# Low parts of more weight slabs made in the first feed-forward stage and kept in DRAM

## Chip, core and metric

The kernel runs on one core of a Trainium2 chip. The metric is the device time of one execution in microseconds; the median of the runs counts. A profile of one execution comes from the hardware profiler. Its engines are called by two names here: PE is TensorE (matmuls), PEld its weight loads, DVE is VectorE, ACT is ScalarE, POOL is GpSimd, and SP is SyncE, whose queue issues all the DMAs (SPq).

## What is computed

Two blocks of two layers each, on 512 tokens of width 1024, all in fp32. A layer of the first block, cut to what matters here:

```python
h = x @ w_in[i]                       # queries, keys, values of three attentions, an index, and gates g
o_fox, o_sb, o_dsa = ...              # forgetting, stick-breaking and top-k attention
gates = sigmoid(g.reshape(b, s, 3, 1024))
merged = gates[:, :, 0] * (o_fox @ w_up_fox[i]) + gates[:, :, 1] * (o_sb @ w_up_sb[i]) + gates[:, :, 2] * (o_dsa @ w_up_dsa[i])
x = layer_norm(ALPHA * x + merged @ w_out[i])
ffn = square(relu(x @ w_ff_in[i])) @ w_ff_out[i]        # 1024 -> 4096 -> 1024
ple = sigmoid(x @ w_ple_gate[i]) * (p[i] @ w_ple[i])
x = layer_norm(ALPHA * x + ffn + ple)
```

The second block (`block2`) has its own `w_in_2` and other mixers. It matters here because part of its weights is prepared during the first block.

## The kernel before, in words

**Three matmuls for one.** Each fp32 operand is split into a high part (the value rounded to the fp32r format that TensorE reads) and a low part (the rest). `mm3` (lines 213 to 215) multiplies high by high, high by low and low by high. A weight slab is 128 partitions x 1024 words, that is four row blocks of 128 by 256 columns, 512 KB. `slab` (line 224) loads it into the tile `raw` on SyncE's queue. `wsplit` (lines 237 and 238) makes the tiles `wh` on ScalarE (a copy that rounds) and `wl` on VectorE (raw less high), or on GpSimd where `lo_on_pool` is set. `raw`, `wh` and `wl` have four buffers each.

**Projections.** `w_tiles` takes output tiles of 128 columns in pairs: two slabs for a pair (the upper and the lower half of the 1024 rows), 24 matmuls of 512 tokens for a tile, and then `emit` does the tile's follow-up work. `wide` does the other kind of product, with four blocks of tokens held in PSUM.

**The order of a layer** (`block1`): `mix1`, `out1`, `ffn`. In `mix1` the string ORDER, 'ISFDftdxBbzy', gives the traced order: index projection (I), scores of the selection (S), projections of the forgetting (F) and of the top-k attention (D), the attentions (f, d, b), the top-k search on VectorE (t), the stick-breaking projection (B), and the three gate branches (x, z, y). The stages I (its second group), D and F have their low parts on GpSimd, by LOP = "iDF". The queries and keys of F and B come through `head_pairs`, the gates through `branch`, both by `w_tiles`. On each engine the framework's scheduler orders the instructions ahead of the run, by traced order and readiness under its own cost estimates; in the run each engine takes its list in that order.

**Low parts in advance.** The feed-forward stage `ffn` runs in four chunks: eight output tiles by `w_tiles` (relu and square, `emit_h`), then the two halves of the second product by `wide`. After each output tile it runs one step of the list `ahead`. A step (`lows2`, lines 256 to 263) loads a slab of the second block's `w_in_2` into `lraw`, copies it to `llo` on ScalarE (line 259), subtracts on GpSimd (line 260) and stores the low part in DRAM (line 263), into a tile of its own. `lraw` and `llo` have two buffers each. `issue_after` puts a step's load behind the latest slab's load in SyncE's queue. There are 24 steps in each of the first block's two layers (one for each layer of the second block), so three of the four chunks carry eight steps and the last none. In the second block `stored` loads the low part from DRAM into `wl` (line 272) where a tile's columns are in the list, and only the high part is computed (line 273).

Of the kernel before, what the change touches and what calls it, by code (L numbers as in the profile page):

```python
# [19 lines left out]
P = 128  # L20
# [3 lines left out]
KD = D // P  # L24
# [45 lines left out]
class Net:  # L70
# [171 lines left out]
        pairs = [[(3352 + j * P, P), (2840 + j * P, P)] for j in range(4)] + [[(1816 + j * 256, 256)] for j in range(2)]  # L242
        return pairs + [[(1304 + j * P, P), (1304 + (j + 2) * P, P)] for j in range(2)] + [[(c + j * 256, 256)] for c in (2328, 3864) for j in range(2)]

    def lows2(self, l):

        nc, w = self.nc, self.a["w_in_2"][l]
        kept = self.lows[l] = {}

        def step(cols, k0):  # L250
            c = sum(n for _, n in cols)
            raw, lo = self.t("lraw", [P, 4, c]), self.t("llo", [P, 4, c], F32R)
            o = 0
            with self.tc.issue_after(self.last_load.ins):
                for c0, n in cols:
                    nc.sync.dma_start(raw[:, :, o:o + n],
                                      w[k0 * P:(k0 + 4) * P, c0:c0 + n].rearrange("(k p) c -> p k c", p=P))
                    o += n
            nc.scalar.activation(lo, raw, AF.Copy)  # L259
            nc.gpsimd.tensor_sub(lo, raw, lo.bitcast(F32))  # L260
            n = self.name("low")
            kept[tuple(cols), k0] = self.dp.tile([P, 4, c], F32, tag=n, name=n)
            nc.sync.dma_start(kept[tuple(cols), k0], lo.bitcast(F32))

        return [lambda cols=cols, k0=k0: step(cols, k0) for cols in self.gates2(l) for k0 in (0, 4)]

    def stored(self, w, cols, k0, nk, lows):

        raw = self.slab(w, cols, k0, nk)
        hi, lo = self.t("wh", raw.shape, F32R), self.t("wl", raw.shape, F32R)  # L270
        with self.tc.issue_after(self.hold):
            self.nc.sync.dma_start(lo.bitcast(F32), lows[tuple(cols), k0])
        self.nc.scalar.activation(hi, raw, AF.Copy)
        return hi, lo

    def w_tiles(self, w, tiles, x, emit, K=KD, lows=None):

        for j0 in range(0, len(tiles), 2):
            pair = tiles[j0:j0 + 2]
            cols = _merge([p for t in pair for p in t])  # L280
            ks = self.KS[self.block]
            if ks == 8:
                raw = self.slab(w, cols, 0, K)
                parts = [[self.wpair(raw[:, :, j * P:(j + 1) * P])] for j in range(len(pair))]
            else:
                slabs = [self.stored(w, cols, k0, ks, lows) if lows else self.wpair(self.slab(w, cols, k0, ks))
                         for k0 in range(0, K, ks)]
                parts = [[(h[:, :, j * P:(j + 1) * P], l[:, :, j * P:(j + 1) * P]) for h, l in slabs] for j in range(len(pair))]
            for j in range(len(pair)):
                ps = self.ps("mm")  # L290
                for k in range(K):
                    h, l = parts[j][k // ks]
                    self.mm3(ps, (h[:, k % ks], l[:, k % ks]), (x[0][:, k], x[1][:, k]), k == 0, k == K - 1)
                emit(j0 + j, ps)
# [305 lines left out]
    def head_pairs(self, w, tiles, x):  # L600


        q, k = {}, {}

        def pair():
            t = self.t("qk", [P, 2, T], F32R)
            return t[:, 0], t[:, 1]

        def emit(i, ps):
            j = i // 2  # L610
            ps = self.staged(ps)
            if i % 2:
                for r in range(2):
                    k[2 * j + r] = pair()
                    self.key_stack(ps, *k[2 * j + r], 64 * r)
                return
            z = pair()
            last = i == len(tiles) - 1
            for r in range(1 if last else 2):
                self.query_stack(ps, z[r], 64 * r, 64 * r)  # L620
                q[2 * j + r] = z[r], z[r]
            if last:
                k[2 * j] = pair()
                self.key_stack(ps, *k[2 * j], 64)

        self.w_tiles(w, tiles, x, emit)
        return q, k

    def forget(self, ffl, b_forget):
# [100 lines left out]
    def branch(self, w, g0, wup, pairs, rows, x, emit):  # L730

        nc = self.nc
        nk = len(pairs)
        full = rows // P
        ups = {}

        def gate(f, ps):
            if f % 2 == 0:
                raw = self.t("raw", [P, nk, 256])
                c = slice(f * P, f * P + 256)  # L740
                nc.sync.dma_start(raw[:, :full], wup[:full * P, c].rearrange("(k p) c -> p k c", p=P))
                h, l = self.t("wh", raw.shape, F32R), self.t("wl", raw.shape, F32R)
                if full < nk:
                    nc.sync.dma_start(raw[:64, full], wup[full * P:, c])
                    self.split(raw[:64, full], h[:64, full], h[64:, full])
                self.wsplit(raw[:, :full], h[:, :full], l[:, :full])
                ups[0] = h, l
            h, l = ups[0]
            s = self.t("sig", [P, T])
            nc.scalar.activation(s, ps, AF.Tanh, scale=0.5)  # L750
            u = self.ps("mm")
            c = slice(f % 2 * P, f % 2 * P + P)
            if full < nk:
                nc.tensor.matmul(u, h[:, full, c], pairs[full][:, 0], start=True, stop=False)
                nc.tensor.matmul(u, h[:, full, c], pairs[full][:, 1], start=False, stop=False)
            for k in range(full):
                self.mm3(u, (h[:, k, c], l[:, k, c]), (pairs[k][:, 0], pairs[k][:, 1]),
                         k == 0 and full == nk, k == full - 1)
            emit(f, s, u)

        self.w_tiles(w, [[(g0 + f * P, P)] for f in range(KD)], x, gate)

    def mix1(self, i, x, then=None):

# [165 lines left out]
    def ffn(self, i, x, y, pt, post=None):  # L930
        nc = self.nc
        a = self.a
        ple = {}
        for j in range(2):
            def emit(b, ps):
                if b == 0:
                    ple[j] = self.wpair(self.slab(a["w_ple"][i], [(j * T, T)], 0, 2))
                wh, wl = ple[j]
                s = self.t("sig", [P, T])
                nc.scalar.activation(s, ps, AF.Tanh, scale=0.5)  # L940
                u = self.ps("mm")
                tok = slice(b * P, (b + 1) * P)
                for k in range(2):
                    self.mm3(u, (pt[0][:, k, tok], pt[1][:, k, tok]), (wh[:, k], wl[:, k]), k == 0, k == 1)
                nc.vector.scalar_tensor_tensor(s, s, 1.0, u, op0=OP.add, op1=OP.mult)
                v = y[b][j]
                nc.vector.scalar_tensor_tensor(v, v, ALPHA, s, op0=OP.mult, op1=OP.add)

            self.wide(a["w_ple_gate"][i], j * T, x, emit, stay=1)
        xo = self.xpair()  # L950
        xn = self.dram([T, D])
        nch = 4
        ahead = self.lows2(i)
        for ch in range(nch):
            hid = []

            def emit_h(f, ps):
                r = self.t("sig", [P, T])
                nc.scalar.activation(r, ps, AF.Relu)
                nc.vector.tensor_mul(r, r, ps)  # L960
                t = self.t("qk", [P, 2, T], F32R)
                self.split(r, t[:, 0], t[:, 1])
                hid.append(t)
                self.run(ahead, 1)

            self.w_tiles(a["w_ff_in"][i], [[(ch * D + f * P, P)] for f in range(KD)], x, emit_h)
            m = _Stack(hid, 0), _Stack(hid, 1)
            last = ch == nch - 1
            if last:
                g, bb = self.bcast(a["ln2_g"][i], D), self.bcast(a["ln2_b"][i], D)  # L970

                st = self.stats()

            def add(j):
                def emit(b, ps):
                    v = y[b][j]
                    nc.vector.tensor_add(v, v, ps)
                    if last:
                        nc.vector.bn_stats(st[b][:, j], v)
                    if last and j == 1:  # L980
                        self.norm_out(y[b], b, st[b], g, bb, 1e-5, xo, xn, post)
                return emit

            self.out_halves(a["w_ff_out"][i][ch * D:(ch + 1) * D], m, add)
        return xo, xn
# [21 lines left out]
    def block1(self, layers=DEPTH, post=None):  # L1007
        self.phase(1, self.FIRST)
        xd = self.a["x"]
        x, rest = self.load_x()  # L1010
        for i in range(layers):
            merged = self.mix1(i, x, None if i else rest)
            if i == 0:
                self.tables = self.rope_tables()
            pt = self.ple_input(i)
            x, y = self.out1(i, merged, xd)
# [672 lines left out]
```

## Time and profile before

| | us |
|---|---|
| median of 3 runs | 2550.74 |
| lowest and highest run | 2550.54, 2554.34 |
| the profiled execution's own time | 2551.98 |
| its span, first to last instruction | 2550.2 |
| TensorE busy in the span | 2472.7 |
| VectorE, ScalarE, GpSimd busy | 1630.3, 1231.7, 729.7 |

The profiled execution is 1.2 us above the median, and its time is 1.8 us longer than its span. All times in the rows below count from the span's start. The stages in that time: the first layer's feed-forward stage proper lies at 486 to 862 us (its first steps are issued at 488.5), the second layer's mixing block at 870 to 1270, its feed-forward stage from about 1372 on, and the second block begins near 1738. TensorE's busy time is modelled from pipelined matmuls, so idle time in it is real, but a busy TensorE isn't always at its peak.

### The profile page before, as it was taken

To read this page: it belongs to the slowest core of one execution; us is meant where nothing else is said; L and a number is where in the kernel's file an instruction comes from. 1 tells how busy PE (TensorE), PEld (TensorE's weight loads), DVE (VectorE), ACT (ScalarE), POOL (GpSimd) and SP (SyncE) were. 2 spreads that over 40 slices of the span, in tenths; PEclk is the share of its full clock that TensorE was granted. 3 is DMA by queue.
4 is the path that set the end of the run, shared out by engine and by line. 5 is a ranking of instruction groups with operands and counts; after the bars stand their busy time and mean duration, and the time that the engine had idled before them with its cause. 6 is when DMAs were issued, how large, how long until landed. Compare 5 with 4: busy or idle time off the path is not lost.

```text
span 2550.2 us, 35074 instructions
## 1 busy us (share of the span) xinstructions
PE 2472.7 (97%) x12660; PEld 2097.7 (82%) x12660; DVE 1630.3 (64%) x3126; ACT 1231.7 (48%) x2271; POOL 729.7 (29%) x845
## 2 busy tenths in 40 slices
PE   8989999999999998999999999998999899999998
PEld 8878888888888887888888888887988688988777
DVE  4985865654344669659465544346699755589874
ACT  5665643344333255665323343233575742576760
POOL 5621560122110264206002122004353312353320
PEclk9999999999999999999999999999999999999999
DMA  5203225366543332132435656334444143554151
GB/s 167 83 16 85 74 83 187 123 197 224 170 161 94 96 85 66 46 86 82 133 119 169 203 190 222 93 97 121 140 143 130 43 150 114 149 153 127 51 178 40
DMA packets 276654, 312.00 MB, mean 122 GB/s; under 512 B 25792, under 2 KB 221696, under 8 KB 276480
## 3 DMA queue, kind: packets, MB, share of 16 engines
q1 hardware_dynamic: 276480, 309.76, 39.4%
q8 instruction: 100, 1.64, 0.3%
q14 instruction: 74, 0.61, 0.1%
HBM read 274.84 MB, written 34.87 MB: 121 GB/s over the span
## 4 chain that ended last, share of the span: by engine, by line
PE 82%; DVE 9%; ACT 3%; DMA 2%; issue 2%; POOL 1%; SPq 0%; DVEq 0%; ACTq 0%; POOLq 0%
PE mm L214 19%; PE mm L215 18%; PE mm L213 18%; PE ss L382 3%; PE av L432 3%; PE ss L214 3%; PE ss L215 3%; PE ss L213 3%; PE tr L417 2%; PE av L215 1%; PE av L214 1%; PE av L213 1%; PE tr L215 1%; PE tr L214 1%; PE tr L213 1%
## 5 line engine op out<-in xcount | busy, mean ns | idle before, releaser
L238 DVE TENSOR_TENSOR wl<-raw,wh 128x1024 fp32r<-128x1024 f32 (+3 forms) x308 | 392.8, 1279 | 326.9 <-ACT wh L237 317.9
L237 ACT ACTIVATE wh<-raw 128x1024 fp32r<-128x1024 f32 (+6 forms) x358 | 361.3, 1013 | 448.8 <-PE tr L215 176.9
L213 PE MATMUL mm<-xt,wh 128*128 128x512 f32 x1456 | 574.4, 394 | 2.1 <-DVE sig L1376 2.1
L215 PE MATMUL mm<-xt,wl 128*128 128x512 f32 x1456 | 572.2, 393 | 2.8 <-DVE wl L238 2.8
L214 PE MATMUL mm<-xt,wh 128*128 128x512 f32 x1456 | 573.8, 394 | 0.0
L215 PEld LDWEIGHTS mm<-xt,wl 128*128 128x128 f32 x1456 | 275.0, 189 | 59.0 <-DVE wl L238 4.4
L213 PEld LDWEIGHTS mm<-xt,wh 128*128 128x128 f32 x1456 | 275.1, 189 | 57.3 <-DVE sig L1376 2.5
L214 PEld LDWEIGHTS mm<-xt,wh 128*128 128x128 f32 x1456 | 274.9, 189 | 54.5 <-issue 0.5
L260 POOL TENSOR_TENSOR llo<-lraw,llo 128x1024 fp32r<-128x1024 f32 x48 | 116.3, 2435 | 378.3 <-ACT llo L259 363.4
L213 PE MATMUL mm<-wh,xt 128*128 128x256 f32 (+6 forms) x624 | 190.4, 311 | 10.1 <-ACT wh L237 8.8
L215 PE MATMUL mm<-wh,xt 128*128 128x256 f32 (+6 forms) x624 | 191.9, 310 | 5.8 <-DVE xt L206 5.7
L214 PE MATMUL mm<-wl,xt 128*128 128x256 f32 (+6 forms) x624 | 192.6, 311 | 2.4 <-DVE wl L238 1.6
L364 POOL TENSOR_SCALAR tiny<-tiny 128x1 f32<-128x1 f32 x24 | 11.9, 495 | 516.7 <-DVE tiny L863 477.7
L391 ACT ACTIVATE s<-s,tm 128x128 f32<-128x128 f32 (+1 forms) x216 | 120.5, 558 | 64.4 <-DVE tm L389 57.2
L214 PE MATMUL mm<-wl,qk 128*128 128x512 f32 x352 | 136.2, 390 | 0.0
L215 PE MATMUL mm<-wh,qk 128*128 128x512 f32 x352 | 136.0, 389 | 0.0
L213 PE MATMUL mm<-wh,qk 128*128 128x512 f32 x352 | 134.7, 389 | 0.0
L394 POOL TENSOR_SCALAR s<-s,tm,kept 128x128 f32<-128x128 f32 (+3 forms) x128 | 78.4, 612 | 195.0 <-DVE tm L393 174.0
L213 PEld LDWEIGHTS mm<-wh,xt 128*128 128x128 f32 x624 | 119.6, 194 | 12.8 <-ACT wh L237 9.2
L215 PEld LDWEIGHTS mm<-wh,xt 128*128 128x128 f32 x624 | 120.4, 193 | 8.3 <-DVE xt L206 7.2
L214 PEld LDWEIGHTS mm<-wl,xt 128*128 128x128 f32 x624 | 120.7, 194 | 5.4 <-DVE wl L238 2.5
L1412 DVE SCALAR_TENSOR_TENSOR acc<-kept,acc 128x511 f32<-128x511 f32 (+6 forms) x168 | 124.1, 739 | 1.6
(373 smaller groups left out, 5256.8 us busy)
## 6 DMA issues: line engine op xcount, KB each, us to landing
raw<-in_w_in SPq DMA_DIRECT2D x84, 512.0 KB, 4.2
raw<-in_w_ff_in SPq DMA_DIRECT2D x64, 512.0 KB, 4.0
raw<-in_w_ff_out SPq DMA_DIRECT2D x64, 512.0 KB, 3.8
raw<-in_w_in SPq DMA_DIRECT2D x104, 256.0 KB, 3.8
low<-llo SPq DMA_DIRECT2D x48, 512.0 KB, 2.8
wl<-low SPq DMA_DIRECT2D x48, 512.0 KB, 3.7
raw<-in_w_out SPq DMA_DIRECT2D x40, 512.0 KB, 3.8
lraw<-in_w_in SPq DMA_DIRECT2D x48, 256.0 KB, 6.1
```

The costliest lines, as they stand in the source:

```text
L213: mm(out, A[0], B[0], start=start, stop=False)
L214: mm(out, A[0], B[1], start=False, stop=False)
L215: mm(out, A[1], B[0], start=False, stop=stop)
L237: self.nc.scalar.activation(hi, raw, AF.Copy)
L238: (self.nc.gpsimd if self.lo_on_pool else self.nc.vector).tensor_sub(lo, raw, hi.bitcast(F32))
L260: nc.gpsimd.tensor_sub(lo, raw, lo.bitcast(F32))
L382: self.nc.tensor.matmul(s, u[:, tok], v[:, :n], start=i == 0, stop=i == len(k) - 1)
L391: nc.scalar.activation(p, p, AF.Exp, bias=m, scale=-1.0, accum_out=den)
L394: nc.gpsimd.tensor_scalar(p, p, r, 1.0 if gate is None else gate, op0=OP.mult, op1=OP.mult)
L417: nc.tensor.transpose(tr[:, kb * P:(kb + 1) * P], p[:, kb * P:(kb + 1) * P], self.ident)
L432: nc.tensor.matmul(av[:, 256 - m.shape[-1]:], v[:, kb], m, start=start and kb + i == 0, stop=stop and kb == n - 1 and i == 1)
L1412: nc.vector.scalar_tensor_tensor(acc[0][:, d:], u[:, :T - d], w[:, k], acc[0][:, d:], op0=OP.mult, op1=OP.add)
```

## The change

The list of steps in the first layer's feed-forward stage is made longer. Ahead of the 24 slabs for the second block come 34 of the first block's own second layer: 17 pairs of output tiles (3 of the forgetting attention's queries and keys, 2 of the stick-breaking attention's, 12 of the gates), two slabs each. After each output tile two steps run instead of one. In the second layer `head_pairs` and `branch` pass the kept low parts to `w_tiles`, which loads them with `stored` instead of making them. The fifth, mixed tile of the stick-breaking queries and keys isn't in the list and is made as before. The first layer and the second layer's own steps stay as they are.

```diff
--- before.py
+++ after.py
@@ -242,10 +242,16 @@
         pairs = [[(3352 + j * P, P), (2840 + j * P, P)] for j in range(4)] + [[(1816 + j * 256, 256)] for j in range(2)]
         return pairs + [[(1304 + j * P, P), (1304 + (j + 2) * P, P)] for j in range(2)] + [[(c + j * 256, 256)] for c in (2328, 3864) for j in range(2)]
 
-    def lows2(self, l):
-
-        nc, w = self.nc, self.a["w_in_2"][l]
-        kept = self.lows[l] = {}
+    def gates1(self):
+
+        pairs = [[(128 * j, 128), (384 + 128 * j, 128)] for j in range(3)]
+        pairs += [[(1158 + 128 * j, 128), (1478 + 128 * j, 128)] for j in range(2)]
+        return pairs + [[(3150 + j * 256, 256)] for j in range(12)]
+
+    def lows_of(self, key, w, columns):
+
+        nc = self.nc
+        kept = self.lows[key] = {}
 
         def step(cols, k0):
             c = sum(n for _, n in cols)
@@ -262,13 +268,13 @@
             kept[tuple(cols), k0] = self.dp.tile([P, 4, c], F32, tag=n, name=n)
             nc.sync.dma_start(kept[tuple(cols), k0], lo.bitcast(F32))
 
-        return [lambda cols=cols, k0=k0: step(cols, k0) for cols in self.gates2(l) for k0 in (0, 4)]
+        return [lambda cols=cols, k0=k0: step(cols, k0) for cols in columns for k0 in (0, 4)]
 
     def stored(self, w, cols, k0, nk, lows):
 
         raw = self.slab(w, cols, k0, nk)
         hi, lo = self.t("wh", raw.shape, F32R), self.t("wl", raw.shape, F32R)
-        with self.tc.issue_after(self.hold):
+        with self.tc.issue_after(self.hold) if self.hold else nullcontext():
             self.nc.sync.dma_start(lo.bitcast(F32), lows[tuple(cols), k0])
         self.nc.scalar.activation(hi, raw, AF.Copy)
         return hi, lo
@@ -283,7 +289,7 @@
                 raw = self.slab(w, cols, 0, K)
                 parts = [[self.wpair(raw[:, :, j * P:(j + 1) * P])] for j in range(len(pair))]
             else:
-                slabs = [self.stored(w, cols, k0, ks, lows) if lows else self.wpair(self.slab(w, cols, k0, ks))
+                slabs = [self.stored(w, cols, k0, ks, lows) if lows and (tuple(cols), k0) in lows else self.wpair(self.slab(w, cols, k0, ks))
                          for k0 in range(0, K, ks)]
                 parts = [[(h[:, :, j * P:(j + 1) * P], l[:, :, j * P:(j + 1) * P]) for h, l in slabs] for j in range(len(pair))]
             for j in range(len(pair)):
@@ -623,7 +629,7 @@
                 k[2 * j] = pair()
                 self.key_stack(ps, *k[2 * j], 64)
 
-        self.w_tiles(w, tiles, x, emit)
+        self.w_tiles(w, tiles, x, emit, lows=self.made)
         return q, k
 
     def forget(self, ffl, b_forget):
@@ -758,7 +764,7 @@
                          k == 0 and full == nk, k == full - 1)
             emit(f, s, u)
 
-        self.w_tiles(w, [[(g0 + f * P, P)] for f in range(KD)], x, gate)
+        self.w_tiles(w, [[(g0 + f * P, P)] for f in range(KD)], x, gate, lows=self.made)
 
     def mix1(self, i, x, then=None):
 
@@ -950,7 +956,9 @@
         xo = self.xpair()
         xn = self.dram([T, D])
         nch = 4
-        ahead = self.lows2(i)
+        ahead = self.lows_of(i, a["w_in_2"][i], self.gates2(i))
+        if i == 0:
+            ahead = self.lows_of("first", a["w_in"][1], self.gates1()) + ahead
         for ch in range(nch):
             hid = []
 
@@ -961,7 +969,7 @@
                 t = self.t("qk", [P, 2, T], F32R)
                 self.split(r, t[:, 0], t[:, 1])
                 hid.append(t)
-                self.run(ahead, 1)
+                self.run(ahead, 1 + (i == 0))
 
             self.w_tiles(a["w_ff_in"][i], [[(ch * D + f * P, P)] for f in range(KD)], x, emit_h)
             m = _Stack(hid, 0), _Stack(hid, 1)
@@ -1009,6 +1017,7 @@
         xd = self.a["x"]
         x, rest = self.load_x()
         for i in range(layers):
+            self.made = self.lows["first"] if i else None
             merged = self.mix1(i, x, None if i else rest)
             if i == 0:
                 self.tables = self.rope_tables()
```

## Rows read from the trace of the kernel before

**Rows 1.** The page: busy time of each engine, and the chain's shares.

```profile
PE 2472.7 (97%) x12660; PEld 2097.7 (82%) x12660; DVE 1630.3 (64%) x3126; ACT 1231.7 (48%) x2271; POOL 729.7 (29%) x845
...
PE 82%; DVE 9%; ACT 3%; DMA 2%; issue 2%; POOL 1%; SPq 0%; DVEq 0%; ACTq 0%; POOLq 0%
```

**Rows 2.** Busy time by stretch, second layer's mixing: us, PE, PEld, DVE, ACT, POOL, clock, DMA share, GB/s.

```profile
920.00:950.00 30.00, 28.89 (x142) 24.51 (x141) 27.14 (x82) 18.49 (x40) 19.41 (x11) 1.00 0.35 97
950.00:980.00 30.00, 30.00 (x142) 26.27 (x141) 29.06 (x73) 20.09 (x36) 21.65 (x18) 1.00 0.24 66
980.00:1000.00 20.00, 16.93 (x96) 13.92 (x94) 19.79 (x51) 12.55 (x31) 10.91 (x18) 0.96 0.39 113
1000.00:1020.00 20.00, 15.52 (x74) 12.77 (x74) 18.83 (x62) 10.76 (x29) 4.33 (x9) 0.78 0.00 0
...
1060.00:1270.00 210.00, 209.86 (x1078) 179.15 (x1077) 139.03 (x249) 112.42 (x224) 53.52 (x83) 1.00 0.34 98
```

**Rows 3.** Busy time by stretch, first feed-forward stage, with the sum of its nine stretches.

```profile
530.00:574.00 44.00, 43.07 (x190) 35.28 (x189) 26.80 (x27) 20.01 (x28) 6.98 (x3) 1.00 0.60 195
574.00:618.00 44.00, 44.00 (x196) 36.42 (x195) 15.40 (x16) 14.45 (x15) 12.10 (x6) 1.00 0.63 204
...
sum 376.00, PE 375.07 PEld 309.98 DVE 180.16 ACT 132.41 POOL 60.41; mean PE 41.67 PEld 34.44 DVE 20.02 ACT 14.71 POOL 6.71
```

**Rows 4.** Line 238 in the first feed-forward stage: durations ns min/median/max, starts, forms.

```profile
L238 DVE TENSOR_TENSOR wl<-raw,wh x68: 1206/1226/3123, 485.5 to 848.0; 128x1024 fp32r<-128x1024 f32 x68
```

**Rows 5.** Line 238 alone by stretch: us, DVE busy, POOL busy, clock, DMA share, GB/s.

```profile
920.00:950.00 30.00, 0.00 (x0) 14.28 (x6) 1.00 0.35 97
...
980.00:1000.00 20.00, 5.25 (x4) 0.00 (x0) 0.96 0.39 113
486.00:862.00 376.00, 93.44 (x68) 0.00 (x0) 1.00 0.52 166
```

**Rows 6.** VectorE in order of time, second layer: start, us, line, operation, tiles.

```profile
928.70 1.36 DVE L672 TENSOR_TENSOR tiny<-tiny,tiny 128x24 f32<-128x24 f32 x1
...
930.38 0.17 DVE L674 TENSOR_TENSOR tiny<-tiny 128x24 f32<-128x24 f32 x1
...
930.84 2.26 DVE L676 TENSOR_SCALAR tiny<-tiny 128x24 f32<-128x24 f32 x1
```

**Rows 7.** The tile of a step's low part: durations ns min/median/max, both layers.

```profile
L259 ACT ACTIVATE llo<-lraw x48: 1058/1062/1067, 495.4 to 1585.5; 128x1024 fp32r<-128x1024 f32 x48
L260 POOL TENSOR_TENSOR llo<-lraw,llo x48: 2387/2405/2960, 496.6 to 1586.7; 128x1024 fp32r<-128x1024 f32 x48
L263 SPq DMA_DIRECT2D low<-llo x48: 338/339/1152, 499.0 to 1589.1; - x48
```

**Rows 8.** DMA issues: count, KB each, median us from issue to landing.

```profile
raw<-in_w_in SPq DMA_DIRECT2D x84, 512.0 KB, 4.2
...
wl<-low SPq DMA_DIRECT2D x48, 512.0 KB, 3.7
...
lraw<-in_w_in SPq DMA_DIRECT2D x48, 256.0 KB, 6.1
```

**Rows 9.** Waits in the first feed-forward stage: us in total, times, longest.

```profile
ACT llo L259 <- DMA lraw<-in_w_in: 74.6, 24, 8.6
...
PE mm L215 <- DVE wl L238: 0.9, 1, 0.9
```

**Rows 10.** ScalarE in order of time, first steps, with the idle time before.

```profile
495.44 1.06 ACT L259 ACTIVATE llo<-lraw 128x1024 fp32r<-128x1024 f32 x1 [8.17 <-DMA lraw<-in_w_in]
...
511.69 1.06 ACT L259 ACTIVATE llo<-lraw 128x1024 fp32r<-128x1024 f32 x1 [8.59 <-DMA lraw<-in_w_in]
```

**Rows 11.** VectorE in order of time, ahead of TensorE's wait at 532 us.

```profile
527.41 2.10 DVE L238 TENSOR_TENSOR wl<-raw,wh 128x1024 fp32r<-128x1024 f32 x1 [0.27 <-ACT wh L237]
529.43 2.88 DVE L947 SCALAR_TENSOR_TENSOR kept<-kept,sig 128x512 f32<-128x512 f32 x1
```

**Rows 12.** Busy time by stretch, second layer's feed-forward stage.

```profile
1400.00:1420.00 20.00, 18.14 (x79) 14.24 (x78) 13.29 (x10) 8.88 (x12) 9.34 (x4) 1.00 0.71 231
```

## The prediction

> **What bounds the kernel now.** I read the page's busy shares and its chain first. TensorE is busy 97% of the span and carries 82% of the chain, VectorE 9% [rows 1]. The change removes no matmul, so it can only give back time in which TensorE stands still, and it loses where it makes TensorE stand still. The views by stretch then show where that is, for the two stages that are edited.
>
> In the second layer's mixing block the place to look at is 920 to 1060 us [rows 2]. From 950 to 980 VectorE is busy 29.06 of 30 us and TensorE still full. From 980 to 1000 VectorE is at 19.79 of 20 and TensorE has 3.07 us idle, from 1000 to 1020 it has 4.48 idle and a granted clock of 0.78, which is worth another 20 x 0.22 = 4.4 us of full-speed work. So some 12 us are lost there, behind a VectorE that was full. From 1060 to 1270, where most gate tiles are computed, TensorE is idle for 0.14 us of 210: a cheaper VectorE buys nothing there.
>
> In the first feed-forward stage TensorE is idle for 0.93 us of 376, all of it between 530 and 574 [rows 3]. That is the stage which gets the new work, and it has little to win and much to lose.
>
> **The change, part by part.**
>
> *Removed in the second layer.* 17 column pairs in two halves make 34 slabs whose low part is no longer computed: 24 of the gates and 4 of the stick-breaking queries and keys on VectorE, 6 of the forgetting attention's on GpSimd. On VectorE that is 28 x 1.23 = 34 us (1226 ns is the median of line 238, [rows 4]), but only what lies ahead of the loss counts. In 980 to 1000 four such subtractions take 5.25 us [rows 5]; three are gates (the fourth is of an up-projection and stays): 3.9 us. The rest lie in the full stretch after 1060 or near it, and I cost them at nothing; what hides them is TensorE's own work, and if that cover went, VectorE with 139 of 210 us [rows 2] would still have room.
>
> On GpSimd six subtractions take 14.28 us between 920 and 950 [rows 5]. While they run, two VectorE instructions on 24 elements take 1.36 and 2.26 us, where their neighbour of the same shape takes 0.17 [rows 6]. Those two alone make (1.36 - 0.17) + (2.26 - 0.17) = 3.3 us of a VectorE that is the chain there. VectorE is full from 920 on (27.14 of 30 us, [rows 2]), and its chain up to 1000 thus shrinks by 3.9 + 3.3, some 7 us. The Trainium skill (SBUF — State Buffer, "SBUF: two separate sides") says that VectorE and GpSimd share one pair of ports under a lock that is held for a whole instruction. The trace agrees with it in these rows; were the two long instructions slow for another reason, only half of the 3.9 us would come back and the sum would end at 2559 in place of 2557.
>
> How much of 7 us reaches TensorE? Nothing, if the attention's own back and forth between four engines is what starves it (VectorE is busy 18.83 of 20 in 1000 to 1020, but waits in turn); all 7, if VectorE's lateness is. VectorE is full in either stretch, and either belongs to attention as well, so I take the middle: **4 us back**, ends 0 and 7.
>
> *Added in the second layer.* 34 loads of low parts, about 0.34 us of SyncE's queue each, as the store [rows 7], landing in 3.7 us [rows 8]. The raw slab of the same tile takes 4.2 us by the same queue [rows 8], so the low part can be there before ScalarE's copy of 1.06 us and VectorE's 1.23 us would have made it. If its buffer comes free late it is 3.7 - 1.06 - 1.23 = 1.4 us later than before, and what queues behind it on SyncE are the next raw slabs. At DMA shares of at most 0.39 [rows 2] I cost them at nothing; the far end is 1.4 us for each of the 17 pairs, 24 us.
>
> *Added in the first feed-forward stage.* 34 steps more, 58 in place of 24: each is a load, a ScalarE copy of 1.06 us, a GpSimd subtraction of 2.41 us and a store [rows 7]. Two are issued for each output tile instead of one. The sums fit: ScalarE 132.4 [rows 3] + 34 x 1.06 = 168.5 of 376 us, GpSimd 58 x 2.41 = 140 us. The DMA share is 0.52 now at 166 GB/s [rows 5], that is 62 MB; 34 x 1.05 MB more make 0.82. What doesn't fit so easily is the order. Each engine runs its list in order. A step's copy holds ScalarE until its load has landed: 74.6 us in 24 steps, 3.1 us each [rows 9], with single holds of 8.17 and 8.59 us [rows 10]. Behind it stand the copies of the slabs that TensorE needs next. A step's store holds SyncE until GpSimd is done, and behind that stand the slabs' loads. With two buffers, two steps cannot follow the two before them sooner than landing, copy and subtraction allow: 6.1 + 1.06 + 2.41 = 9.6 us [rows 7, 8]. TensorE works 24 matmuls on each tile, which at 44 us for 196 [rows 3] are 5.4 us. So the steps no longer come eight to a chunk of the stage with rest before the next chunk, but fill it to its end.
>
> TensorE's 0.93 us fell in the first eight steps: it waits for a low part [rows 9], and ahead of that one VectorE needs 2.10 us for another and 2.88 us for a sum [rows 11], in place of 1.23 for the first. By the rule of the Trainium skill named above, which here speaks against the change, these are waits for GpSimd's subtractions, which the change makes more than twice as many; the price that follows contains them. The second layer's first eight steps cost 1.86 us [rows 12]. The eights behind them cost nothing, since each began with a full lead. Without the rests that lead isn't rebuilt, so I price all 58 steps as those eight: 58 x 0.93 / 8 = 6.7 to 58 x 1.86 / 8 = 13.5 us, less the 0.93 already paid: 5.8 to 12.6, and I take **9 us lost**. The near end is 0: at the mean hold, 58 x 3.1 = 180 us with 168.5 busy leave ScalarE 28 us of 376. The far end is that each of 29 pairs holds ScalarE for the longest 8.6 us [rows 9]: 249 + 168.5 - 376 = 42 us.
>
> *Moved.* The 24 steps for the second block come after the 34 new ones, still inside the stage by their issue (29 of 32 tiles); their readers belong to the second block. The second layer's own feed-forward stage keeps one step for a tile. Both cost nothing.
>
> **Sum.** Against the profiled execution of 2551.98 us: + 9 - 4 = 2557. It ran 1.2 us above the median of 2550.74, so the median comes to **2556 us**.
>
> **The rivals.**
>
> *VectorE's relief wins (not slower).* Place: 920 to 1020 us. The whole 7 us come back and the clock's dip with it in part, while the feed-forward stage hides its steps as the later eights are hidden now. For: VectorE is full ahead of the loss [rows 2]. Against: a denser schedule than today's has no row that stayed free. It decides where a hold of ScalarE stays at its mean of 3.1 us. 2550.7 - 7 = 2544.
>
> *Both vanish.* The steps hide, and attention's own chain keeps TensorE waiting: 2551. For it speaks that two of three eights of steps cost nothing.
>
> *ScalarE and SyncE are held throughout.* Half of the far end of 42 us: 2550.7 + 21 = 2572. For: holds of 8 us follow each other in the first eight [rows 10]. Against: a ScalarE that is late finds its load landed, and the hold shrinks.
>
> *The low parts arrive late in the second layer.* From 1060 on TensorE has no slack, and 8 pairs of gates lie there: 8 x 1.4 = 11 us on top, 2562 with no other loss. It decides if buffers, not loads, are what the stage waits for.
>
> *It doesn't do what it says*: a key that isn't found falls back to computing. The tiles' columns, as merged, are those of the list, so I give it nothing.
>
> **Numbers.** Forecast 0.42 (its own range 2552 to 2562), relief 0.22, both vanish 0.20, held throughout 0.10, late low parts 0.06. A change under 0.2% (5.1 us) can hardly be told from none, and the forecast's own range lies across that edge (2555.8): 0.13 of it counts as the same. Faster is the relief: 0.22. Same is both vanish and that 0.13: 0.33. Slower is the rest: 0.45. The range from 2543 to 2572 leaves out the low third of the relief and the high half of the held case.
>
> **What would show it.** Right: in the first feed-forward stage GpSimd at about 140 us of subtractions spread to the end, TensorE idle there by some 9 us in several places with a release by a low part or a slab's copy, and 980 to 1020 with less than 7.55 us idle. Wrong: a feed-forward stage at 1 us idle (the lead does hold), or 980 to 1020 unchanged (VectorE wasn't the cause), or waits for loaded low parts after 1060.

## The result, and the profile after

The changed kernel takes 2569.82 us (median of 4 runs, 2566.24 to 2574.59), against 2552.40 for the kernel before (median of 4). The ratio is 1.0066 [1.0054, 1.0078], so it is slower by 17 us. Forecast was 2556, the forecast's own range ended at 2562 and the whole range at 2572: the sign and the whole range hold, the size doesn't. The measured time lies beside the rival "held throughout" (2572, chance 0.10). The profiled execution took 2566.24 us, with a span of 2564.5, which is 14.3 us longer than the span before. It is the fastest of the four, and the others have a granted clock lower by 0.002 to 0.005.

The page of the changed kernel, busy times and the chain's shares [rows 1]:

```profile
PE 2478.7 (97%) x12660; PEld 2101.2 (82%) x12660; DVE 1626.2 (63%) x3098; ACT 1264.2 (49%) x2305; POOL 796.0 (31%) x873
...
PE 82%; DVE 9%; DMA 3%; ACT 3%; issue 2%; POOL 1%; SPq 0%; DVEq 0%; ACTq 0%; POOLq 0%
```

The shares hardly move; DMA has gone from 2% to 3% of the chain. The stretches tell more. The changed kernel's second-layer mixing, busy time by stretch (us, PE, PEld, DVE, ACT, POOL, clock, DMA share, GB/s). It lies some 14 us later than in [rows 2], so the stretches are shifted by that:

```profile
934.00:964.00 30.00, 30.00 (x151) 26.27 (x150) 25.84 (x89) 21.52 (x45) 8.82 (x7) 1.00 0.63 202
964.00:994.00 30.00, 30.00 (x143) 26.17 (x142) 28.60 (x72) 19.33 (x35) 19.25 (x17) 1.00 0.23 66
994.00:1014.00 20.00, 19.16 (x114) 16.23 (x112) 18.72 (x57) 15.27 (x39) 9.02 (x18) 1.00 0.58 191
1014.00:1034.00 20.00, 15.52 (x90) 12.44 (x91) 18.66 (x59) 11.34 (x30) 4.37 (x9) 1.00 0.09 32
1074.00:1284.00 210.00, 207.59 (x1060) 177.11 (x1059) 110.96 (x216) 110.63 (x218) 48.05 (x79) 1.00 0.48 151
...
1126.00:1166.00 40.00, 37.59 (x208) 33.42 (x207) 21.61 (x36) 26.29 (x53) 7.85 (x16) 1.00 0.34 102
```

The first stretch has lost its 1.11 us of idle TensorE, the third has 0.84 idle in place of 3.07, and the granted clock of the fourth is 1.00 (the 2.4 GHz level throughout) in place of 0.78. That is the relief: 3.3 us less idle time in the four stretches (5.32 in place of 8.66), and a clock dip of 0.04 and 0.22 of 20 us each, 5.2 us, that is gone. The last two lines are a new loss: the long stretch has 2.41 us idle where there was 0.14, all of it between 1126 and 1166.

The first feed-forward stage of the changed kernel in the same view [rows 3]; the four stretches that aren't shown are full, as the first line is:

```profile
530.00:574.00 44.00, 44.00 (x196) 36.46 (x195) 28.86 (x22) 24.41 (x32) 22.25 (x10) 1.00 0.87 290
574.00:618.00 44.00, 37.90 (x157) 29.97 (x156) 21.94 (x19) 16.07 (x17) 17.87 (x8) 0.96 0.80 262
...
662.00:706.00 44.00, 42.17 (x185) 34.27 (x184) 19.43 (x19) 17.47 (x19) 18.27 (x8) 1.00 0.77 243
...
750.00:794.00 44.00, 41.62 (x183) 33.76 (x181) 18.10 (x17) 16.08 (x17) 16.11 (x7) 1.00 0.79 256
794.00:838.00 44.00, 42.61 (x188) 34.81 (x187) 28.87 (x26) 20.85 (x28) 10.47 (x5) 1.00 0.64 215
...
sum 376.00, PE 364.30 PEld 298.51 DVE 205.06 ACT 162.90 POOL 141.84; mean PE 40.48 PEld 33.17 DVE 22.78 ACT 18.10 POOL 15.76
```

TensorE is idle for 11.7 us of 376 (0.93 before), plus a dip of the clock to 0.96 in 574 to 618. Up to 574, where the first 16 steps run, nothing is lost. The loss comes where one chunk of the stage gives way to the next, near 590 to 613, 701 and 775 to 796. The waits of this stage in the changed kernel (us in total, times, longest), against [rows 9]:

```profile
ACT llo L265 <- DMA lraw<-in_w_in: 146.0, 52, 8.6
...
PE mm L215 <- DVE wl L238: 4.2, 3, 1.4
PE mm L213 <- ACT wh L237: 4.1, 4, 1.8
...
PE mm L214 <- DVE wl L238: 3.4, 2, 1.8
```

ScalarE's hold on the steps' loads has gone from 74.6 to 146.0 us, and TensorE now waits for slabs of the stage's own weights.

**Where the 14.3 us lie.** For each point of the trace before I took the time at which another trace has put the same number of matmul columns through TensorE; the growth of that difference over a stage is the stage's loss. The table has all kernels of this study, in us of the profiled executions; negative is a gain, and the stages are given by their times before. What is left over lies in other stretches. It is largest, some 3 us, in e10 and e12, ahead of 200 us, where their code and TensorE's order are those of the kernel before. A stage can lose more than its idle time: the clock's dip counts, and a TensorE that is counted as busy around a wait moves fewer columns. The 0.93 us of idle time before were worth 1.4 us in this measure.

| kernel | feed-forward 1, 482 to 889 | mixing, 889 to 1140 | 1140 to 1179 | feed-forward 2, 1253 to 1437 | second block | span |
|---|---|---|---|---|---|---|
| the change | +15.9 | -8.6 | +2.7 | -1.3 | +5.6 | +14.3 |
| e1_cost | +15.6 | -1.1 | +0.5 | +0.8 | -3.3 | +12.3 |
| e2_gain | +0.4 | -8.6 | +4.2 | -1.4 | +2.5 | -3.2 |
| e3_nohold | -0.9 | -8.6 | +4.2 | -2.5 | +0.8 | -7.9 |
| e4_nolock | -0.6 | -8.6 | +4.3 | -2.5 | +4.8 | -2.4 |
| e5_dve | +1.3 | -8.7 | +4.3 | -2.5 | +7.2 | +1.9 |
| e6_before_nohold | -0.6 | +0.9 | 0.0 | -2.6 | -0.4 | -2.8 |
| e7_few | -0.9 | -8.6 | 0.0 | -2.5 | +0.4 | -11.8 |
| e8_bufs | +14.0 | -8.7 | +4.2 | +4.7 | +0.6 | +15.1 |
| e9_few_act | +10.0 | -8.7 | +0.5 | +0.4 | +0.4 | +3.6 |
| e10_fox | -1.4 | -4.8 | 0.0 | -2.6 | +3.6 | -2.1 |
| e11_gates | -0.4 | -1.7 | 0.0 | -2.5 | +4.7 | +0.8 |
| e12_no_sb | -1.5 | -8.7 | +4.2 | -2.5 | +0.3 | -5.0 |

The verdict of a kernel is its median, given below; the table says only where one execution differs. For the change, the two terms that the forecast priced, the first two columns, come to +7.3; the next three bring 7.0 more.

### The profile page after: what moved, and what is told of

The parts are those of the page before. It is cut to its first block, busy times and chain, and to the rows that moved or that the text cites. A ratio compares the mean times of both kernels' runs of the same rounds, so it can differ in the third digit from the quotient of the medians.

```text
span 2564.5 us, 35372 instructions
## 1 busy us (share of the span) xinstructions
PE 2478.7 (97%) x12660; PEld 2101.2 (82%) x12660; DVE 1626.2 (63%) x3098; ACT 1264.2 (49%) x2305; POOL 796.0 (31%) x873
## 4 chain that ended last, share of the span: by engine, by line
PE 82%; DVE 9%; DMA 3%; ACT 3%; issue 2%; POOL 1%; SPq 0%; DVEq 0%; ACTq 0%; POOLq 0%
PE mm L214 19%; PE mm L215 19%; PE mm L213 19%; PE ss L388 3%; PE ss L213 3%; PE ss L214 3%; PE ss L215 3%; PE av L438 2%; DMA lraw<-in_w_in 2%; PE tr L423 1%; PE av L215 1%; PE av L214 1%; PE av L213 1%; PE tr L215 1%; PE tr L214 1%
## 5 line engine op out<-in xcount | busy, mean ns | idle before, releaser
L238 DVE TENSOR_TENSOR wl<-raw,wh 128x1024 fp32r<-128x1024 f32 (+3 forms) x280 | 373.3, 1340 | 297.9 <-ACT wh L237 287.6
L237 ACT ACTIVATE wh<-raw 128x1024 fp32r<-128x1024 f32 (+6 forms) x324 | 323.4, 1007 | 357.0 <-PE tr L215 141.7
L266 POOL TENSOR_TENSOR llo<-lraw,llo 128x1024 fp32r<-128x1024 f32 x82 | 200.2, 2446 | 395.0 <-ACT llo L265 387.7
L213 PE MATMUL mm<-wh,xt 128*128 128x256 f32 (+6 forms) x624 | 193.2, 316 | 10.6 <-ACT wh L237 8.6
L215 PE MATMUL mm<-wh,xt 128*128 128x256 f32 (+6 forms) x624 | 195.0, 315 | 4.2 <-DVE xt L206 4.1
L265 ACT ACTIVATE llo<-lraw 128x1024 fp32r<-128x1024 f32 x82 | 86.9, 1060 | 223.7 <-DMA lraw<-in_w_in 220.3
L213 PEld LDWEIGHTS mm<-wh,xt 128*128 128x128 f32 x624 | 122.5, 199 | 13.4 <-ACT wh L237 9.0
L215 PEld LDWEIGHTS mm<-wh,xt 128*128 128x128 f32 x624 | 123.6, 199 | 6.5 <-DVE xt L206 5.4
```

Source lines behind the costliest of these rows:

```text
L213: mm(out, A[0], B[0], start=start, stop=False)
L215: mm(out, A[1], B[0], start=False, stop=stop)
L238: (self.nc.gpsimd if self.lo_on_pool else self.nc.vector).tensor_sub(lo, raw, hi.bitcast(F32))
```

## The experiments

Diffs are against the changed kernel unless another is named. The kernels came in three groups, each timed beside the kernel before: e1 to e4 (2553.33 us), e5 to e8 (2552.90), e9 to e12 (2553.20).

### Cost and gain apart: e1_cost, e2_gain

e1 keeps the 58 steps, and the second layer computes its own low parts:

```diff
-            self.made = self.lows["first"] if i else None
+            self.made = None
```

> The 58 steps of the first feed-forward stage stay, the second layer computes all its low parts itself again. If the loss is the steps' alone, the feed-forward stage is as in the changed kernel (TensorE idle about 11.7 us of 390, against 0.9 before) and 994 to 1034 us falls back to what the kernel before lost there (7.5 us idle and a dip of the clock): some 7 us above the changed kernel, 2575 us. If the loss came from the loads in the second layer, it is near the kernel before, 2552.

2564.30 us, 1.0054 [1.0035, 1.0072]. The feed-forward stage loses 15.6 us, as in the change, and there is no relief in the mixing. The whole is even 5.5 us below the change, where 7 above it was expected: the table has 8.9 us less in the second block, and 2.2 less near 1150.

e2 leaves the 34 steps out and lets the second layer load one tile of other data from DRAM in place of the low parts:

```diff
-            ahead = self.lows_of("first", a["w_in"][1], self.gates1()) + ahead
+            self.lows["first"] = {(tuple(cols), k0): self.blank() for cols in self.gates1() for k0 in (0, 4)}
...
-                self.run(ahead, 1 + (i == 0))
+                self.run(ahead, 1)
```

> The 34 steps are left out and the second layer loads its low parts from one DRAM tile that holds other data, so its output is not the reference's. If the loads relieve VectorE, about 8 us come back between 920 and 1020 us and the whole is 2544 to 2547; if attention's own chain is what starves TensorE, 2551. If the second block loses time by a new order of its instructions alone, up to 6 us of the gain are lost again there.

2548.91 us, 0.9982 [0.9973, 0.9992]. The stage loses nothing (+0.4), the mixing gains 8.6 and gives back 4.2 near 1150. So the loss is in making the low parts, and the relief is twice the 4 us that were forecast.

### Hold or lock: e3_nohold, e4_nolock, e5_dve

A step can cost TensorE time in two ways: its copy holds ScalarE until a load lands, and its subtraction on GpSimd slows VectorE. e3 moves the copy to GpSimd, so ScalarE waits for no step. (The edits of e3, e4 and e5 reach the steps of both layers.)

```diff
-            nc.scalar.activation(lo, raw, AF.Copy)
+            nc.gpsimd.tensor_copy(lo, raw)
```

> The steps' copy moves from ScalarE to GpSimd, so ScalarE never waits for a step's load; GpSimd holds its ports for longer. If ScalarE's holds make the loss, the feed-forward stage loses under 4 us in place of some 16 and the whole is about 2556; if VectorE's waits for GpSimd make it, the stage loses 16 us or more, 2570 to 2585.

2546.49 us, 0.9975 [0.9964, 0.9985]: 23 us below the change with the same steps, 16.8 of them in this stage by the table. e4 keeps the copy on ScalarE and leaves out the subtraction, so that the rounded copy is stored in place of the low part:

```diff
-            nc.gpsimd.tensor_sub(lo, raw, lo.bitcast(F32))
```

> The steps' subtraction on GpSimd is left out in both layers (what is stored is the rounded copy, not the low part). ScalarE still waits for the step's load. If VectorE's waits for GpSimd make the loss, the feed-forward stage loses under 4 us and the whole is about 2555; if the holds of ScalarE make it, it loses 10 us or more, 2563 to 2570. The shorter cycle of the two buffers can move some of the holds.

2544.41 us, 0.9968 [0.9954, 0.9981]. e5 has the subtraction on VectorE, in whose list it then stands, so that GpSimd has no part in the steps:

```diff
-            nc.gpsimd.tensor_sub(lo, raw, lo.bitcast(F32))
+            nc.vector.tensor_sub(lo, raw, lo.bitcast(F32))
```

> The changed kernel with the steps' subtraction on VectorE in both layers; GpSimd has no subtraction left in the feed-forward stages, ScalarE still makes the copy and waits for its load. If ScalarE's holds suffice for the loss, the first feed-forward stage loses 10 us or more and the whole is 2563 to 2570. If the loss needs a hold and a VectorE that GpSimd delays, the stage loses under 3 us: 2546 to 2552.

2553.70 us, 0.9999 [0.9988, 1.0009]. The sums of the same nine stretches, 486 to 862, of e3, of e4 (with its first stretch ahead) and of e5:

```profile
sum 376.00, PE 376.00 PEld 311.40 DVE 222.25 ACT 110.39 POOL 228.61; mean PE 41.78 PEld 34.60 DVE 24.69 ACT 12.27 POOL 25.40
```

```profile
486.00:530.00 44.00, 44.00 (x195) 36.43 (x195) 19.68 (x25) 19.00 (x22) 0.00 (x0) 1.00 1.00 317
...
sum 376.00, PE 376.00 PEld 311.44 DVE 162.16 ACT 164.82 POOL 3.37; mean PE 41.78 PEld 34.60 DVE 18.02 ACT 18.31 POOL 0.37
```

```profile
sum 376.00, PE 374.85 PEld 308.54 DVE 223.83 ACT 164.06 POOL 1.68; mean PE 41.65 PEld 34.28 DVE 24.87 ACT 18.23 POOL 0.19
```

In e3 TensorE is idle for nothing, though GpSimd works 228.61 us there: the subtractions alone do no harm. In e4 it is idle for nothing either, though ScalarE still waits for the steps' loads:

```profile
ACT llo L265 <- DMA lraw<-in_w_in: 108.4, 52, 8.8
```

So the hold alone does no harm, nor does a DMA share of 1.00 at 317 GB/s. e5, with a hold of 109.1 us, has 1.15 idle. Only both together cost 14 to 16 us. The hold is then longer as well, 146.0 in place of 108.4, but that is not what it takes: e8 below has both, with a hold of only 103.3 us, and loses 14.0. Nor is it how long VectorE works in all: it is busy for 222 and 224 us in e3 and e5, and for 205 us in the change.

Where the two meet can be read at the first change of chunk. The changed kernel in order of time, ScalarE's, SyncE's, GpSimd's and VectorE's rows one after another (start, us, line, operation, tiles, idle time before):

```profile
576.24 0.63 ACT L204 ACTIVATE qk<-sig 128x512 fp32r<-128x512 f32 x1 [2.86 <-DVE sig L968]
576.77 2.94 ACT L237 ACTIVATE wh<-raw 128x1024 fp32r<-128x1024 f32 x3
587.00 1.06 ACT L265 ACTIVATE llo<-lraw 128x1024 fp32r<-128x1024 f32 x1 [7.28 <-DMA lraw<-in_w_in]
588.50 1.06 ACT L265 ACTIVATE llo<-lraw 128x1024 fp32r<-128x1024 f32 x1 [0.45 <-DMA lraw<-in_w_in]
589.47 1.04 ACT L237 ACTIVATE wh<-raw 128x1024 fp32r<-128x1024 f32 x1
...
609.31 1.99 ACT L237 ACTIVATE wh<-raw 128x1024 fp32r<-128x1024 f32 x2
...
575.63 0.37 SPq L224 DMA_DIRECT2D raw<-in_w_ff_out  x1
579.11 1.50 SPq L224 DMA_DIRECT2D raw<-in_w_ff_in  x2
580.66 1.72 SPq L262 DMA_DIRECT2D lraw<-in_w_in  x2
...
588.13 4.70 POOL L266 TENSOR_TENSOR llo<-lraw,llo 128x1024 fp32r<-128x1024 f32 x2 [13.61 <-ACT llo L265]
...
590.54 3.38 DVE L238 TENSOR_TENSOR wl<-raw,wh 128x1024 fp32r<-128x1024 f32 x1 [6.48 <-ACT wh L237]
```

And the same moment in e4, whose TensorE is within 0.4 us of the changed kernel's at 555:

```profile
564.67 0.63 ACT L204 ACTIVATE qk<-sig 128x512 fp32r<-128x512 f32 x1 [1.40 <-DVE sig L967]
...
583.75 1.06 ACT L237 ACTIVATE wh<-raw 128x1024 fp32r<-128x1024 f32 x1 [0.66 <-PE tr L215]
...
602.36 1.99 ACT L237 ACTIVATE wh<-raw 128x1024 fp32r<-128x1024 f32 x2
...
569.73 5.81 SPq L224 DMA_DIRECT2D raw<-in_w_ff_in  x2
```

The first row of either fence is the last follow-up copy of the chunk's eight output tiles. It ends 11.6 us later in the changed kernel. The copies `wh` of waiting slabs stand behind it and then run three in a row. The buffers of `raw` come free late, and SyncE asks for the next chunk's slabs at 579.11 in place of 569.73. Two more steps' loads stand behind these in its queue. ScalarE waits for them until 587.00 and comes to the next `wh` at 589.47, 5.7 us later than in e4. By the order of loads and copies, this is the last slab of the chunk's own second product, asked for at 575.63. VectorE's subtraction behind it takes 3.38 us instead of 1.2, while GpSimd is at its two from 588.13 on, and TensorE stands for 3.55 us in two pieces from 588.8 on. Four more copies of steps follow, each behind its load, and ScalarE comes to the next chunk's first two slabs at 609.31, in e4 at 602.36. There TensorE stands for another 2.56 us. The two add up to the 6.1 us of idle time in 574 to 618.

Why the copies fall behind in the first place is seen in the line's durations. Line 238 (`wl`) from 486 to 578, ns min/median/max, in the changed kernel and in e4:

```profile
L238 DVE TENSOR_TENSOR wl<-raw,wh x17: 1211/1226/3412, 485.2 to 577.9; 128x1024 fp32r<-128x1024 f32 x17
```

```profile
L238 DVE TENSOR_TENSOR wl<-raw,wh x18: 1217/1226/1226, 485.5 to 573.9; 128x1024 fp32r<-128x1024 f32 x18
```

Without GpSimd's subtractions no `wl` takes over 1.23 us; with them some take up to 3.4, and VectorE is busy 205.06 us of the stage in place of 162.16. The Trainium skill's rule of the shared ports (SBUF — State Buffer, "SBUF: two separate sides") agrees with this. A follow-up copy (line 204) waits for VectorE, and then a step's copy holds ScalarE, in turn, so both delays add up over 16 steps: from 486 to 578 ScalarE waits for VectorE's part of the follow-up for 10.3 us and for the steps' loads for 39.1, in e4 for 3.8 and 31.2. The losing kernel e1 shows the same times as the change, within 1.5 us (577.40 for the last copy, 580.27 for the slabs, 590.95 for `wh`):

```profile
577.40 0.63 ACT L204 ACTIVATE qk<-sig 128x512 fp32r<-128x512 f32 x1 [2.86 <-DVE sig L968]
...
590.95 1.04 ACT L237 ACTIVATE wh<-raw 128x1024 fp32r<-128x1024 f32 x1
...
580.27 1.77 SPq L224 DMA_DIRECT2D raw<-in_w_ff_in  x2
```

### Buffers: e8_bufs

```diff
-        1: dict(raw=4, ... lraw=2, llo=2),
+        1: dict(raw=4, ... lraw=3, llo=3),
```

> The changed kernel with three buffers in place of two for the steps' load and for their low part. If ScalarE's holds come from loads that the two buffers let start too late, the feed-forward stage loses under 6 us: 2553 to 2560. If the order on ScalarE alone makes them, the time stays at 2565 to 2572.

2564.15 us, 1.0039 [1.0025, 1.0053]. The hold shrinks to 103.3 us, but the stage still loses 14.0. The first change of chunk is milder (the last copy at 568.93, slabs at 571.80, 2.67 us idle); the later ones lose as much and dip the clock. e8's stretches:

```profile
662.00:706.00 44.00, 41.27 (x175) 33.43 (x174) 16.56 (x16) 15.34 (x15) 19.09 (x8) 0.96 0.83 266
...
750.00:794.00 44.00, 40.89 (x175) 32.88 (x174) 16.40 (x15) 16.72 (x17) 19.08 (x8) 0.97 0.75 249
```

A third buffer lets the loads start earlier; the order of ScalarE's list stays, and so does the loss. The second layer's stage, whose 24 steps have the third buffer too, loses 4.7.

### The same step in the kernel before: e6_before_nohold

The edit of e3, made to the kernel before.

> The kernel before with the steps' copy on GpSimd, 24 steps in each layer and no low parts loaded in the second layer. The 0.9 and 1.9 us idle at the start of the two feed-forward stages go: 2549 to 2551, some 3 us below the kernel before. If all that the copy's move gave over it were its own, 2546; then the loads in the second layer are worth nothing.

2548.64 us, 0.9981 [0.9972, 0.9990]. The gain of 4 us lies in the second layer's feed-forward stage (-2.6), which had [rows 12], and in the first's 0.93 us of [rows 3]. So of e3's 7 us against the kernel before some 3 to 4 belong to steps that were there already.

### Fewer steps: e9_few_act, e7_few

If only what lies ahead of 1020 is worth making, the forgetting attention's 3 pairs and the first gate branch's 4 suffice, 14 steps in place of 34. e9 makes these and leaves the copy on ScalarE; e7 has it on GpSimd too:

```diff
         pairs = [[(128 * j, 128), (384 + 128 * j, 128)] for j in range(3)]
-        pairs += [[(1158 + 128 * j, 128), (1478 + 128 * j, 128)] for j in range(2)]
-        return pairs + [[(3150 + j * 256, 256)] for j in range(12)]
+        return pairs + [[(3150 + j * 256, 256)] for j in range(4)]
```

> The 14 steps of the smaller list with the copy on ScalarE, as in the changed kernel. Two steps a tile now end half way through the second chunk but one. If the loss goes with the chunk starts that steps reach, two of three are still met and the stage loses 8 to 11 us; with the relief of some 9 us the whole is about 2552. If the smaller list alone makes the gain, it equals the one with the copy on GpSimd: 2541.

2555.53 us, 1.0007 [0.9997, 1.0016]. Its steps end at 700, and so does its loss, at two changes of chunk in place of three (the whole is 3.5 us above the 2552 that were expected):

```profile
574.00:618.00 44.00, 40.03 (x163) 31.74 (x162) 20.57 (x18) 16.46 (x18) 18.23 (x8) 0.92 0.82 250
...
662.00:706.00 44.00, 41.13 (x181) 33.43 (x180) 16.97 (x17) 17.18 (x18) 17.75 (x7) 1.00 0.71 236
706.00:750.00 44.00, 44.00 (x196) 36.45 (x195) 22.07 (x27) 17.13 (x23) 0.00 (x0) 1.00 0.41 129
```

> The copy on GpSimd, and of the 17 pairs only the forgetting attention's three and the first branch's four gates, 14 steps in place of 34. If only low parts computed ahead of 1020 us matter, the whole relief of some 8 us stays: 2544 to 2547, as with all 34. If the steps for the other 20 slabs buy something after 1060 us, it is 2 to 4 us slower than with all 34. The 4 us that are lost near 1150 us go, if the stick-breaking attention's loads make them.

**2540.65 us, 0.9948 [0.9935, 0.9960]**: the best of the study, 12 us below the kernel before and 29 below the change. e7's stretches in the mixing and the sum in the feed-forward stage:

```profile
998.00:1018.00 20.00, 15.75 (x91) 12.72 (x92) 18.24 (x58) 11.47 (x29) 4.73 (x9) 1.00 0.13 39
1128.00:1168.00 40.00, 39.86 (x240) 36.19 (x239) 34.51 (x58) 28.71 (x67) 23.63 (x38) 1.00 0.24 70
...
sum 376.00, PE 376.00 PEld 311.37 DVE 208.94 ACT 110.33 POOL 153.71; mean PE 41.78 PEld 34.60 DVE 23.22 ACT 12.26 POOL 17.08
```

The whole relief of 8.6 us is there with 14 of 34 low parts, and the loss near 1150 is not.

### Which low parts give what: e10_fox, e11_gates, e12_no_sb

All three have the copy on GpSimd. e10 keeps the forgetting attention's pairs alone, e11 the first branch's 4 gate pairs alone, and e12 drops only the stick-breaking pairs. The lists' part of e10's edit:

```diff
-        pairs += [[(1158 + 128 * j, 128), (1478 + 128 * j, 128)] for j in range(2)]
-        return pairs + [[(3150 + j * 256, 256)] for j in range(12)]
+        return pairs
```

> The copy on GpSimd, and only the forgetting attention's three pairs, 6 steps. By the prediction's terms GpSimd's six subtractions held up VectorE for 3.3 of 7 us, so it keeps about half of the relief: 2544 to 2546. If GpSimd's part is all of it: 2541.

> The copy on GpSimd, and only the first branch's four gate pairs, 8 steps. By the prediction's terms three subtractions on VectorE, 3.9 of 7 us: 2544 to 2546. If the gates are nothing: 2549, as the kernel before with the copy moved.

> The copy on GpSimd, all 34 but the stick-breaking attention's four, 30 steps. If its loads make the 4 us lost near 1150 us, they go and it is 2541 to 2543; if the gates of the second and third branch make them, the loss stays and it is 2546.

e10 2548.98, 0.9984 [0.9974, 0.9993]; e11 2546.88, 0.9975 [0.9965, 0.9985]; e12 2546.65, 0.9968 [0.9955, 0.9981]. One row each of e10, e11 and e12 that decides:

```profile
998.00:1018.00 20.00, 13.74 (x83) 10.56 (x83) 19.79 (x64) 11.91 (x32) 5.54 (x10) 1.00 0.00 0
```

```profile
998.00:1018.00 20.00, 15.20 (x76) 11.70 (x77) 18.06 (x61) 11.17 (x31) 5.52 (x11) 0.88 0.00 0
```

```profile
1128.00:1168.00 40.00, 37.67 (x218) 34.12 (x217) 27.66 (x49) 26.31 (x61) 16.80 (x32) 0.96 0.35 112
```

The forgetting attention's pairs give 4.8 us, the gates alone 1.7, both together 8.6: more than the sum. The medians agree on the last: against e6, which has the copy's move and no low parts, e10 is level, e11 gains 2 us and e7 8. That e10's own gain doesn't show there was not expected (2544 to 2546); its profiled execution loses 3.1 us ahead of 200 us and 3.6 in the second block. With e10's pairs alone VectorE is still at 19.79 of 20, so the next gates stand in the way; with e11's alone the clock still dips to 0.88. e12 has the loss near 1150 as e3 has it, and e7, e10 and e11 don't. So it comes with the low parts of the second and third gate branches, and not with the stick-breaking pairs. How these cause it isn't settled. An order of TensorE's list is the nearest candidate, not tried by itself: between 1060 and 1270 it differs from the kernel before in 391 to 394 of 1076 matmuls in every kernel with this loss, and in 0 to 132 in those without. Waiting loads are not it: of the changed kernel's TensorE waits in 1074 to 1284 none names a loaded `wl`; the longest is for the stick-breaking attention's start on GpSimd, 1.5 us.

## Why the forecast was right in sign and short in size

**Bound and direction.** That time counts only where TensorE loses it, and that the stage with the new work has little to win and much to lose, held: 15.9 us lost against 8.6 gained. Both terms were sized too small, and the two errors nearly cancel: +7.3 measured, +5 forecast, which is luck. What carries the profiled execution to +14.3 is the 7.0 us of stretches that were costed at nothing.

**The feed-forward term was mis-sized: 9 forecast, 15.9 measured** (15.6 in e1, where it stands alone). The step that failed is "I price all 58 steps as those eight". By that the first steps would have lost as before, and each later eight the same. In fact the first 16 steps lose nothing, and even the old 0.93 us are gone. The loss isn't paid by the step but by the chunk: lateness of ScalarE grows over a chunk's eight tiles and is paid at the change of chunk, at the last slab of one and the first slabs of the next. The text had the parts of this (ScalarE's holds, GpSimd's lock, SyncE's queue, "without the rests that lead isn't rebuilt"), but not the place, which was to be found from when the next chunk's slabs are asked for. It took the lock as paid ("the price that follows contains them") and the long hold as the rival's; e3 to e5 show that neither costs much without the other.

**The relief was mis-sized: 4 forecast, 8.6 measured.** The place was right. What failed is not "I take the middle": TensorE's idle time from 920 to 1020 fell from 8.66 to 5.32 us, so 3.3 us of it came back, near the middle of 0 and 7. The sum left out the clock. The text had priced its dip from 1000 to 1020 at 4.4 us and then gave it to a rival alone; the granted clock went from 0.96 and 0.78 to 1.00, worth 0.8 + 4.4 = 5.2 us, and with the 3.3 that makes 8.5. The effect on VectorE that was forecast is there: the instruction on 24 elements that took 2.26 us in [rows 6] (line 676 there, line 682 now) takes 0.17:

```profile
942.74 0.17 DVE L682 TENSOR_SCALAR tiny<-tiny 128x24 f32<-128x24 f32 x1
```

The 4.8 us of e10 stand beside the 3.3 us that were worked out for it, but they don't confirm them: e10's TensorE is idle for 7.49 us from 918 to 1018, only 1.2 less than before, and the clock is full, so most of the gain is the clock's. The forecast test "980 to 1020 with less than 7.55 us idle" came out at 0.84 + 4.48 = 5.32, with a full clock. The other signs came too: GpSimd at 141.84 us in the stage, and TensorE idle in several places, released by a low part or a slab's copy.

**Costed at nothing, and not nothing.** The loads after 1060 never hold TensorE up, as said, but the gates that were thought free of effect bring 2.7 us of loss near 1150 (4.2 to 4.3 in e2 to e5, e8 and e12). The second block, whose code is unchanged, lost 5.6 us in the profiled execution. The scheduler orders its instructions differently after an edit upstream: of the last 4300 matmuls, 814 stand in another place than before. The column swings from -3.3 to +7.2 between kernels whose second block has the same code. Kernels that share one order there, on all four engines, can be set side by side: the change and e5 (+5.6, +7.2), e3 and e4 (+0.8, +4.8), e2 and e8 (+2.5, +0.6), e7 and e9 (+0.4, +0.4), and with the order of the kernel before e1 and e6 (-3.3, -0.4). With one order the values lie up to 4 us apart, so some of it is chance; the change's order has the two highest, so some of it is likely order. Executions of one kernel differ as well (e11's profiled one is 5.9 us above its median). How the 5.6 divides wasn't tried and stays open.

**The rivals.** "ScalarE and SyncE are held throughout" named the nearest mechanism, at 21 us, and the time came out beside it. Holds of 146 us were measured, and e4 shows that they cost TensorE nothing without the lock. "Relief wins" (2544) is what e3 is, at 2546.49: it was a matter of one engine for the copy. "Late low parts" did not occur as a wait for loads.

## What to carry to other kernels

A copy that waits for a background load should not stand in the in-order list of the engine that feeds the critical one; put it on an engine with slack, even a slow one. Here the hold did harm only together with a second delay, on VectorE, and a test that removed only one of them would have put the blame on that one. Of work made in advance keep only what lies ahead of a stretch that loses time: 14 of 34 low parts gave all of the gain. And when a stage is loaded more, look for the loss where its phases change, by when the next phase's loads are asked for.

## What the runs showed of the hardware that was not expected

GpSimd's rounding copy of 128x1024 is as quick as ScalarE's (1062 ns, [rows 7]), while its subtraction of the same shape takes 2.3 times as long. Tile `llo` of e3, ns min/median/max:

```profile
L265 POOL CAST llo<-lraw x82: 1037/1042/2109, 495.4 to 1584.0; 128x1024 fp32r<-128x1024 f32 x82
L266 POOL TENSOR_TENSOR llo<-lraw,llo x82: 2386/2402/3482, 499.4 to 1587.4; 128x1024 fp32r<-128x1024 f32 x82
```

And 16 DMA engines busy for a whole stretch of 44 us (e4, 317 GB/s, 486 to 530) did not make TensorE wait once. Why not wasn't tried.
